# A seventh pair of up tiles through seven half products, with its weight sums kept in DRAM, and three moves in VectorE's order

## The chip, the cores and the metric

The kernel runs on one NeuronCore of a Trainium2 chip. TensorE (PE) multiplies into PSUM, VectorE (DVE) and ScalarE (ACT) work on PSUM and SBUF, GpSimd (POOL) scales the softmax, and SyncE (SP) issues nearly all DMAs. The metric is the device time of one execution in microseconds (us), the median of several runs.

## What is computed

One layer: forgetting attention on 512 tokens of width 1024 with 16 heads, a layer norm, a gated MLP of inner width 2816 with a causal convolution of three taps on its gate, a second layer norm, and a gated per-layer embedding. Everything is float32. The part that the change touches most is the MLP:

```python
def conv_ffn(x, w_up, conv_w, conv_b, w_down):
    u, g = jnp.split(x @ w_up, [FFN_DIM], axis=-1)
    g = causal_dwconv(g, conv_w, conv_b)
    return (jax.nn.gelu(g, approximate=False) * u) @ w_down
```

and, for the two smaller edits, the softmax of attention: `pr = softmax(q k^T * scale + c_q - c_k)` under a causal mask, then `pr @ v`.

## The kernel before

**Precision.** Each float32 operand is cut into a high and a low part (`whi`, `wlo` for weights; ACT makes the high part at line 123, DVE the low part at line 129), and each product is three matmuls (`three`, line 147). The class `Weights` (line 64) holds a list of units of up to 128x1024 weights in the order of use. A call `W.get(i, ahead)` cuts the units up to `i + ahead` and starts loads behind them; in the MLP `ahead` is 4, so DVE's work on a unit stands in its order four units ahead of the unit's matmuls. Raw weights rotate through four buffers, cut ones through five.

**The MLP.** The 22 tiles of inner width (`f`) come in 11 pairs (`j`). A plain pair makes, for each of its two tiles, the gate `g` and the up product `u` with 24 matmuls of 512 columns each (`up`, line 704); `conv` (line 714) follows on the gate, `product` (line 724) on both. A pair in `UP_PAIRS` is made by Winograd's form of Strassen's algorithm (`up_step`, line 751): seven products of halves instead of eight, for `g` (s = 0) and for `u` (s = 1), in four steps. Steps 0, 1 and 2 have 24 matmuls of 256 columns for each s, step 3 has 12. At step 0 ACT copies one product to a side buffer (`c1`) and zeroes its half bank, and DVE adds the two products (line 781); step 1 accumulates into that bank, so it waits for this add. `conv_product` (line 798) does both convolutions and both products after step 3.

The form needs sums and differences of blocks of the weights. For pairs not in `KEPT` they are made when the weights are cut: `t12` (two subtractions of 128x512, lines 207 and 208), `t3` and `t4` (one each, lines 215 and 222). For pairs in `KEPT` they are made during attention, written to DRAM and read back: `keep_load` (line 399) writes a finished set and loads the next raw blocks, `keep_sums` (line 413) makes four subtractions on DVE. There are two such rounds for a pair. They stand before the first head and behind `scores(h)` of even heads.

**Down products.** The down product goes by the same algorithm over groups of three pairs (`PAIRS`): part 0 is pairs 0 to 2, part 1 is 3 to 5, part 2 is 6 to 8; the rest is done plainly. While part p's up tiles are made, the down product of part p-1 runs in slices, called here d0 to d11 (`down`, line 825). Three slices make a phase: d0 to d2 use rows of the three pairs for the banks x and y, d3 to d5 and d6 to d8 use sums for z and x, d9 to d11 use one block for x. A slice has 12 matmuls of 512 columns (six in the last phase). At the end of a phase DVE adds the finished banks into `y` (`give`, line 849; two adds to a bank), and x is free for the next phase after that. `between` (line 875) takes the next slices: in parts 1 and 2 one at each of four places in a pair, in part 3 in turn two and one (`CHUNKS`, line 32). In a pair made of halves these places are behind step 0 of g, step 0 of u, step 1 and step 2.

The down product needs sums of a pair's products (`operand_sums`, four DVE additions, lines 814 to 817) and their high and low parts (`operand_parts`, three ACT copies and three DVE subtractions, lines 822 and 823: `a`, `b` and `s`). If the next pair is in `APART` (line 40), these are put into the next pair: the sums into step 0 of u ahead of its add, the parts behind it.

**Order.** From tile 2 on, DVE and ACT keep the order of the program text (`manual_schedule`, line 883). PE and SP are ordered by the compiler, which takes ready instructions out of the text's order. Ahead of that, in attention, DVE is ordered by the compiler as well, but `keep_sums` is tied behind the last mask instruction and the masks of odd heads behind the last sum (`issue_after`, lines 418 and 486).

**PSUM.** Six banks (`six`) serve the down product, two (`two`) the up tiles from tile 6 on. So a gate of tile f+1 waits until `conv(f)` has read the gate of tile f.

**Attention.** The loop at line 582 runs over h. Each turn has the scores of head h, a projection for a later head, the transposes P^T of head h-1 (`turn`, line 503; DVE writes the low part `PTl` at line 516) and the values of head h-2 (`values`). The layer's input `y` is loaded at h = 14, into the buffer that the last projection frees.

Of the kernel before, what the change touches and what calls it, by code (L numbers as in the profile page):

```python
# [19 lines left out]
H = 16  # L20
# [10 lines left out]

CHUNKS = (None, (1,) * 12, (1,) * 12, (2, 1) * 4)

UP_PAIRS = (2, 3, 4, 6, 7, 9)

KEPT = (3, 4, 6, 7)

DMA_PAIRS = (1, 2)

APART = (2, 3, 4, 7)  # L40
HALF = S // 2
ALPHA = 2.0 ** 0.25
EPS = 1e-5
# [99 lines left out]
def trunk_layer(ctx: ExitStack, tc: tile.TileContext, xT, x2d, pT, wqk, wv0, wv1, wv2, bf, wo, wup, cwb,  # L143
# [112 lines left out]
    for part in range(4):  # L256
# [3 lines left out]
        for i in range(2 * len(fs)):  # L260
            f, q = fs[i // 2], i % 2
            j, n = f // 2, i % 4
            if j in UP_PAIRS:
                stages = up_units(j)
# [4 lines left out]
            for _ in range(CHUNKS[part][i] if part else 0):  # L269
                if todo:  # L270
                    src, c, make = todo.pop(0)
                    u_dn[part - 1].append(W.add(src, n=c, inner=512, make=make))
            if j in UP_PAIRS and n == 3:
                for sq in range(2):
# [124 lines left out]
    def keep_load():  # L399

        if made:
            to, ab = made.pop()
            for n, t in enumerate(ab):
                nc.sync.dma_start(to[:, 2 * n:2 * n + 2, :], t.rearrange("p (a b) -> p a b", b=512))
        if to_keep:
            (j, q), to = to_keep.pop(0)
            ab = (ap.tile([P, UNIT], F32, name=f"ka{j}_{q}", tag="keep", bufs=1),
                  base.tile([P, UNIT], F32, name=f"kb{j}_{q}", tag="raw", bufs=RAW_BUFS))
            for n, t in enumerate(ab):
                nc.sync.dma_start(t.rearrange("p (a b) -> p a b", b=P), wup[2 * j + n, 1 - q])  # L410
            in_work.append((to, ab))

    def keep_sums():

        if in_work:
            behind = ExitStack()
            if last_mask:
                behind.enter_context(tc.issue_after(last_mask[0]))
            to, ab = in_work.pop()
            b11, b21, b12, b22 = [t[:, c:c + 512] for t in ab for c in (0, 512)]  # L420
            nc.vector.tensor_sub(b11, b12, b11)
            nc.vector.tensor_sub(b12, b22, b12)
            nc.vector.tensor_sub(b22, b22, b11)
            last_sum[:] = [nc.vector.tensor_sub(b21, b21, b22).ins]
            behind.close()
            made.append((to, ab))
# [91 lines left out]
    def values(h):  # L518
        m, j2 = divmod(h, 2)
        th, tl = PTh[h % 2], PTl[h % 2]  # L520
        ps = bank(f"o{h}")
        for j in range(NT):
            q0, o, w = PT[j]
            for n, p in enumerate((th, tl)):
                nc.tensor.matmul(ps[:, q0:], V[:, j, h], p[:, o:o + w], start=j == 0 and n == 0,  # L525
                                 stop=j == NT - 1 and n == 1)
        a = slice(j2 * 64, j2 * 64 + 64)
        if j2 == 0:
            outs[m] = ap.tile([P, S], F32, tag="o", name=f"o_{m}", bufs=1)
        o = outs[m]  # L530
        nc.scalar.activation(o[a], ps[64:], AF.Copy)
        nc.vector.tensor_add(o[a], ps[:64], o[a])
        if j2 == 1:
            nc.scalar.activation(oh[:, m, :], o, AF.Copy)
            nc.vector.tensor_sub(ol[:, m, :], o, oh[:, m, :].bitcast(F32))
# [46 lines left out]
    for h in range(H + 2):  # L582
        m, s = divmod(h, 2)
        if h == 2:
            project(2, 0)
        if h < H:
            scores(h)

            if s == 0:
                keep_sums()  # L590
                keep_load()
        if m + 1 < KD and h != 2:
            project(m + 1, s)
        for k in OUT_FIRST.get(h, ()):
            out_first(k)
        if s == 1 and h + 1 < H:
            stack(h + 1)
        if 1 <= h < H + 1:
            turn(h - 1)
        if h >= 2:  # L600
            values(h - 2)
        if s == 1 and h + 1 < H:
            stack(h + 2)
        if h == H - 2:
            y = base.tile([P, NT, D], F32, tag="xh", name="y")
            for t in range(NT):
                nc.sync.dma_start(y[:, t, :], x2d[t * P:(t + 1) * P, :])
# [96 lines left out]
    def up(f, s, c=slice(0, S), amid=None):  # L704
        if (f, s) not in ups:
            ups[f, s] = bank(f"{'gu'[s]}{f}", "two" if f >= 6 else None)
        hi, lo = W.get(u_up[f, s], 4 if f > 1 else 2)
        for k in range(KD):
            w = slice(k * P, (k + 1) * P)
            three(ups[f, s][:, c], hi[:, w], lo[:, w], x1h[:, k, c], x1l[:, k, c], k == 0, k == KD - 1)  # L710
            if amid is not None and k == 3:
                flip(*amid)

    def conv(f):

        pg = ups.pop((f, 0))
        a = gates[f] = hpool.tile([P, S], F32, tag="a", name=f"a{f}", bufs=2)
        nc.scalar.activation(a, pg, AF.Identity, bias=cw[:, f, 3:4], scale=cw[:, f, 2:3])
        nc.vector.scalar_tensor_tensor(a[:, 1:], pg[:, :S - 1], cw[:, f, 1:2], a[:, 1:],
                                       op0=ALU.mult, op1=ALU.add)  # L720
        nc.vector.scalar_tensor_tensor(a[:, 2:], pg[:, :S - 2], cw[:, f, 0:1], a[:, 2:],
                                       op0=ALU.mult, op1=ALU.add)
# [148 lines left out]
    for part in range(4):  # L871
        ops = []
        slots = iter(CHUNKS[part] or ())

        def between():
            for _ in range(next(slots, 0)):
                next(before)

        for f in range(6 * part, min(6 * part + 6, NF)):
            q, j = f % 2, f // 2  # L880
            if f == 2:

                ordered.enter_context(tc.manual_schedule(
                    engines={mybir.EngineType.DVE, mybir.EngineType.Activation}))
            if q == 0 and j not in APART:
                E = hpool.tile([P, 8 * HALF], F32, tag="E", name=f"E{j}")
            if f == 0:
                a, b = slice(0, HALF), slice(HALF, S)
                up(0, 0, a)
                up(0, 1, a)  # L890
                up(1, 0, a, (3, x1h, x1l, xt))
                up(0, 0, b)
                up(0, 1, b)
                up(1, 0, b)
                conv(0)
                product(0, E[:, :S])
                continue
            if j in UP_PAIRS:
                if q == 0:
                    up_step(j, 0, 0, E)  # L900
                    between()
                    up_step(j, 0, 1, E, (lambda: operand_sums(E)) if j in APART else None)
                    if j in APART:
                        operand_parts(pending.pop(), E)
                        E = hpool.tile([P, 8 * HALF], F32, tag="E", name=f"E{j}")
                    between()
                    continue
                for st in (1, 2):
                    up_step(j, st, 0, E)
                    up_step(j, st, 1, E)  # L910
                    if st == 1:
                        between()
                between()
                up_step(j, 3, 0, E)
                up_step(j, 3, 1, E)
                conv_product((f, f - 1), E)
            else:
                if f > 1:
                    up(f, 0)
                conv(f)  # L920
                between()
                up(f, 1)
                product(f, E[:, q * S:(q + 1) * S])
            if f == 1:
                x_sums()
            if q:
                if part < 3:
                    ops.append([cut_tiles("A", 2, 3, f"a{j}"), cut_tiles("B", 1, 5, f"b{j}", pool=hpool),
                                cut_tiles("S", 4, 4, f"s{j}")])
                    if j + 1 in APART:  # L930
                        pending.append(ops[-1])
                    else:
                        operand_sums(E)
                        operand_parts(ops[-1], E)
                else:
                    h, l = cut_tiles("S", 4, 4, f"s{j}")
                    e = E[:, :2 * S].rearrange("p (a b) -> p a b", b=HALF)
                    last_cut[:] = [nc.scalar.activation(h, e, AF.Copy).ins]
                    nc.vector.tensor_sub(l, e, h.bitcast(F32))
                    ops.append((h, l))  # L940
            if j not in UP_PAIRS:
                between()
        if part < 3:
            before = down(part, ops)
# [127 lines left out]
```

## Time and profile before

| | |
|---|---|
| Three runs | 653.12 to 653.72 us, median 653.72 |
| The profiled execution | 653.87 us; its span in the trace 652.1 us |
| PE, PE weight loads | 644.8 us busy (99%), 568.7 us (87%) |
| DVE, ACT, POOL | 521.2 us (80%), 367.3 us (56%), 93.0 us (14%) |
| DMA | 109.56 MB, mean 168 GB/s |
| Longest groups on DVE | low parts of weights, 90 of 128x1024, 109.7 us |

A timeline row has start, duration, engine, line, operation, tile out and in, and in brackets the idle time ahead of it and what ended it. Durations of rows that follow each other on one engine overlap a little, so start to start is the better measure of what an instruction costs its engine. The chain of waits is the work that ended last, followed back from the end; a row there has start, duration, engine, tile and line.

In this execution pair 7 ends on PE at 467.82, tiles 16 and 17 (pair 8, plain) run with d8 to d11 until 497.06, and pair 9 (halves, sums made on DVE) with d0 to d5 of the next part until 533.62.

### The profile page before, as it was taken

The numbers are of one execution on the slowest core, as the hardware profiler recorded it, in microseconds if no ns is written. First come the engines' busy times: TensorE is split into PE (matmuls) and PEld (weight loads), VectorE is DVE, ScalarE is ACT, GpSimd is POOL, SyncE is SP. The second block draws the span as 40 slices with busy tenths as digits, with TensorE's granted clock in tenths as the row PEclk, the third lists the DMA queues.
The fourth block names the chain that finished last, engine by engine and source line by source line (L and its number), as shares of the span: only waits on it lengthen the run. The fifth ranks groups of instructions, "written<-read, shape, count | busy, mean of one in ns | idle before, by whom it ended". The sixth has DMA issues, their size and how long they took to land.

```text
span 652.1 us, 10003 instructions
## 1 busy us (share of the span) xinstructions
PE 644.8 (99%) x3666; PEld 568.7 (87%) x3666; DVE 521.2 (80%) x854; ACT 367.3 (56%) x643; POOL 93.0 (14%) x85
## 2 busy tenths in 40 slices
PE   8999999999999999999999999999999999999997
PEld 8899888888888889889999988999978998888886
DVE  6764789988886599857899887799788998599464
ACT  6643777877785326946657564646545554425231
POOL 0000554454455021110000000000000000011000
PEclk9999999999999999999999999999999999999999
DMA  8763554555586215675655546564644473551321
GB/s 293 238 232 131 206 205 160 178 187 149 184 268 238 87 57 160 130 198 179 191 192 178 178 133 208 170 193 123 227 135 156 149 228 99 189 191 40 132 80 50
DMA packets 45858, 109.56 MB, mean 168 GB/s; under 512 B 4400, under 2 KB 8240, under 8 KB 45808
## 3 DMA queue, kind: packets, MB, share of 16 engines
q1 hardware_dynamic: 44944, 105.77, 49.6%
q0 software_dynamic: 864, 3.15, 2.6%
q8 instruction: 29, 0.48, 0.3%
q14 instruction: 21, 0.17, 0.1%
HBM read 96.19 MB, written 10.49 MB: 164 GB/s over the span
## 4 chain that ended last, share of the span: by engine, by line
PE 92%; DVE 4%; ACT 1%; issue 1%; DMA 1%; SPq 0%; DVEq 0%; ACTq 0%
PE u L152 16%; PE g L152 16%; PE pp L152 14%; PE x L152 7%; PE gt L152 7%; PE pv L152 7%; PE r L152 3%; PE z L152 3%; PE ap L152 3%; PE ao L152 3%; PE o L525 3%; PE t L512 2%; PE y L152 2%; PE s L475 2%; PE pl L152 2%; PE s L477 1%
## 5 line engine op out<-in xcount | busy, mean ns | idle before, releaser
L123 ACT ACTIVATE whi<-raw 128x1024 fp32r<-128x1024 f32 (+4 forms) x135 | 125.6, 938 | 92.5 <-PE pv L152 13.7
L129 DVE TENSOR_TENSOR wlo<-raw,whi 128x1024 fp32r<-128x1024 f32 (+4 forms) x130 | 138.3, 1073 | 33.8 <-ACT whi L123 32.8
L499 POOL TENSOR_SCALAR pr<-pr,rl 128x128 f32<-128x128 f32 (+1 forms) x64 | 74.9, 1186 | 132.8 <-DVE rl L495 132.8
L638 POOL TENSOR_TENSOR mv<-mv,neghalf 128x1 f32<-128x1 f32 x8 | 11.6, 1445 | 347.8 <-DVE mv L637 324.1
L152 PE MATMUL g<-x1h,whi 128*128 128x256 f32 (+1 forms) x168 | 54.5, 324 | 0.0
L152 PE MATMUL g<-x1l,whi 128*128 128x256 f32 (+1 forms) x168 | 54.4, 324 | 0.0
L152 PE MATMUL g<-x1h,wlo 128*128 128x256 f32 (+1 forms) x168 | 54.3, 323 | 0.0
L152 PE MATMUL u<-x1l,whi 128*128 128x256 f32 (+1 forms) x160 | 52.9, 331 | 0.0
L152 PE MATMUL u<-x1h,wlo 128*128 128x256 f32 (+1 forms) x160 | 52.9, 331 | 0.0
L152 PE MATMUL u<-x1h,whi 128*128 128x256 f32 (+1 forms) x160 | 52.9, 331 | 0.0
L152 PE MATMUL pp<-xh,wlo 128*128 128x512 f32 x128 | 50.6, 395 | 0.8 <-DVE PTl L516 0.8
L152 PE MATMUL pp<-xl,whi 128*128 128x512 f32 x128 | 50.0, 391 | 0.0
L152 PE MATMUL pp<-xh,whi 128*128 128x512 f32 x128 | 50.0, 391 | 0.0
L491 ACT ACTIVATE pr<-s,nm 128x128 f32<-128x128 f32 (+1 forms) x64 | 33.6, 528 | 10.4 <-DVE nm L487 10.3
L152 PEld LDWEIGHTS g<-x1l,whi 128*128 128x128 f32 x168 | 32.0, 190 | 2.7
L152 PEld LDWEIGHTS g<-x1h,whi 128*128 128x128 f32 x168 | 31.9, 190 | 2.7
L152 PEld LDWEIGHTS g<-x1h,wlo 128*128 128x128 f32 x168 | 31.9, 190 | 2.5
L152 PEld LDWEIGHTS u<-x1h,whi 128*128 128x128 f32 x160 | 30.4, 190 | 3.0
L152 PEld LDWEIGHTS u<-x1l,whi 128*128 128x128 f32 x160 | 30.4, 190 | 3.0
L152 PEld LDWEIGHTS u<-x1h,wlo 128*128 128x128 f32 x160 | 30.4, 190 | 2.8
L487 DVE CUSTOM_DVE_ANT_0 s<-s,mask 128x128 f32<-128x128 f32 (+1 forms) x64 | 30.0, 512 | 1.7 <-PE s L477 1.5
L123 ACT ACTIVATE whi<-side 128x512 fp32r<-128x512 f32 (+1 forms) x33 | 25.5, 782 | 9.7 <-PE u L152 3.6
(550 smaller groups left out, 1820.2 us busy)
## 6 DMA issues: line engine op xcount, KB each, us to landing
raw<-wup SPq DMA_DIRECT2D x34, 512.0 KB, 3.5
raw<-wdn SPq DMA_DIRECT2D x23, 512.0 KB, 3.9
raw<-wqk SPq DMA_DIRECT2D x16, 512.0 KB, 3.4
ka<-wup SPq DMA_DIRECT2D x8, 512.0 KB, 3.9
kb<-wup SPq DMA_DIRECT2D x8, 512.0 KB, 3.4
kept<-kb SPq DMA_DIRECT2D x8, 512.0 KB, 3.5
kept<-ka SPq DMA_DIRECT2D x8, 512.0 KB, 3.1
raw<-wo SPq DMA_DIRECT2D x8, 512.0 KB, 4.1
```

The source lines that it names most:

```text
L123: self.nc.scalar.activation(hi[:, c:e], piece, AF.Copy)
L129: self.nc.vector.tensor_sub(lo[:, c:e], piece, hi[:, c:e].bitcast(F32))
L152: nc.tensor.matmul(ps, lhsT, rhs, start=start and n == 0, stop=stop and n == 2, skip_group_check=on)
L475: nc.tensor.matmul(ps[:, :n], QA[:, q], KA[:, :n], start=True, stop=False)
L477: nc.tensor.matmul(ps[:, :n], qb[0:68, q], kb[0:68, :n], start=False, stop=True)
L487: last_mask[:] = [nc.vector.tensor_tensor_reduce(ps[:, :w], ps[:, :w], mask[:, S - w:], -1.0, BIG, op0=ALU.add, op1=ALU.min, accum_out=nm[ ...
L491: nc.scalar.activation(pr[:, off:off + w], ps[:, :w], AF.Exp, bias=nm[:, i:i + 1], scale=-1.0, accum_out=ls[:, i:i + 1])
L499: nc.gpsimd.tensor_scalar_mul(pr[:, off:off + w], pr[:, off:off + w], rl[:, i:i + 1])
L512: nc.tensor.transpose(ps[:, w:w + P], pr[:, o:o + P], ident)
L525: nc.tensor.matmul(ps[:, q0:], V[:, j, h], p[:, o:o + w], start=j == 0 and n == 0, stop=j == NT - 1 and n == 1)
L638: nc.gpsimd.tensor_tensor(mv[:, 3:4], mv[:, 2:3], neghalf, op=ALU.pow)
```

## The change

Pair 8 (tiles 16 and 17, the last pair of part 2) joins `UP_PAIRS` and `KEPT`. Pairs 8 and 9 join `APART`, so the sums and parts of pair 7 stand in pair 8 and those of pair 8 in pair 9. Two more rounds of sums are kept: the sums of the first new one stand at h = 14, and `keep_sums` and `keep_load` are called once more at h = 16, where the load of `y` now stands too. For h = 2 the round moves from behind the scores to behind `turn` and `values`. And in a plain tile whose slice ends a phase, `conv` stands behind that slice and its adds into `y`. With pair 8 gone from the plain ones, this holds for tile 10 alone (slice d8 of part 1); tile 11 has d10, and tiles 20 and 21 of part 3 have d6, d7 and d9, d10 there.

```diff
-UP_PAIRS = (2, 3, 4, 6, 7, 9)
+UP_PAIRS = (2, 3, 4, 6, 7, 8, 9)
-KEPT = (3, 4, 6, 7)
+KEPT = (3, 4, 6, 7, 8)
-APART = (2, 3, 4, 7)
+APART = (2, 3, 4, 7, 8, 9)
...
-            if s == 0:
+            if s == 0 and h != 2:
                 keep_sums()
                 keep_load()
...
         if h >= 2:
             values(h - 2)
+        if h in (2, H):
+            keep_sums()
+            keep_load()
         if s == 1 and h + 1 < H:
             stack(h + 2)
-        if h == H - 2:
+        if h == H:
             y = base.tile([P, NT, D], F32, tag="xh", name="y")
...
-                conv(f)
+
+                n = 4 * (j - 3 * part) + 2 * q
+                late = part and any(sum(CHUNKS[part][:n], i) % 3 == 2 for i in range(CHUNKS[part][n]))
+                if not late:
+                    conv(f)
                 between()
+                if late:
+                    conv(f)
                 up(f, 1)
```

## The prediction

> **What bounds the kernel now.** I read the page's busy shares first, then the stretches of the MLP around pair 8, then the chain of waits, then DVE's timeline.
>
> ```profile
> PE 644.8 (99%) x3666; PEld 568.7 (87%) x3666; DVE 521.2 (80%) x854; ACT 367.3 (56%) x643; POOL 93.0 (14%) x85
> 467.84:475.80 7.96, 7.96 (x36) 6.57 (x35) 6.45 (x13) 4.49 (x8) 0.00 (x0) 1.00 0.32 105
> 475.80:497.06 21.26, 20.86 (x93) 16.97 (x92) 16.79 (x24) 9.70 (x13) 0.00 (x0) 1.00 0.62 194
> 497.06:505.40 8.34, 8.34 (x51) 7.38 (x50) 8.12 (x13) 5.29 (x9) 0.00 (x0) 1.00 0.25 72
> 505.40:513.90 8.50, 8.50 (x63) 8.01 (x62) 8.39 (x15) 4.46 (x8) 0.00 (x0) 1.00 0.65 191
> 513.90:533.62 19.72, 19.72 (x133) 18.27 (x133) 19.45 (x29) 10.23 (x15) 0.00 (x0) 1.00 0.60 198
> ```
>
> A stretch has its length, then busy us of PE, weight loads, DVE, ACT and POOL, then granted clock, DMA share and GB/s. The kernel is bound by PE, and PE's clock is full (1.00). But the last three rows, pair 9, show a second limit: there DVE is busy for 35.96 of 36.56 us. Fewer matmuls help only where DVE still serves PE in time. In pair 8 (the two rows before) DVE has 29.22 - 23.24 = 6.0 us to spare.
>
> **Matmuls of pair 8.**
>
> ```profile
> 466.36 1.46 PE u L152 x12
> 490.26 5.44 PE u L152 x24
> 497.06 2.87 PE g L152 x24
> 532.18 1.44 PE u L152 x12
> 508.28 1.39 PE x L152 x6
> 509.66 1.36 PE y L152 x6
> 481.40 0.61 DVE y L627
> 482.05 1.64 PE x L152 x6
> 483.69 5.21 PE g L152 x23
> ```
>
> These are rows of the chain. Plain, the pair is 4 x 5.44 = 21.76 us. As halves it is 6 x 2.87 + 2 x 1.44 = 20.10 us: **-1.66**. The slices d8 to d11 are five runs of six (1.36 each, 6.8 us) either way. So 21.76 + 6.8 = 28.56 us of matmuls took 497.06 - 467.82 = 29.24 us: 0.68 us is lost where x of d9 waits for the add into `y` of d8 (481.40, then 482.05).
>
> The Trainium skill, "TensorE: Matmul & The Clock Gate", section "Back-to-back issue gap", gives an isolated gap of N/2.4 + 2.5 ns; by it the 168 half matmuls against 96 whole ones would save an estimated 2.4 us. The rows (0.120 and 0.227 us a matmul) decide for the smaller saving.
>
> **DVE behind pair 7, in pair 8.** DVE keeps the text's order, so its queue can be written out.
>
> ```profile
> 468.96 0.75 DVE L719 SCALAR_TENSOR_TENSOR a<-E,cw,a 128x511 f32<-128x511 f32 x1 [0.93 <-ACT a L718]
> 473.71 0.42 DVE L814 TENSOR_TENSOR E<-E 128x256 f32<-128x256 f32 x1
> 475.19 0.69 DVE L823 TENSOR_TENSOR a7l<-E,a7h 128x512 fp32r<-128x512 f32 x1
> 477.54 0.68 DVE L222 TENSOR_TENSOR raw<-raw,side 128x512 f32<-128x512 f32 x1
> 478.14 1.22 DVE L129 TENSOR_TENSOR wlo<-side,whi 128x1024 fp32r<-128x1024 f32 x1
> 479.28 0.74 DVE L719 SCALAR_TENSOR_TENSOR a<-g,cw,a 128x511 f32<-128x511 f32 x1
> 480.72 0.68 DVE L129 TENSOR_TENSOR wlo<-raw,whi 128x512 fp32r<-128x512 f32 x1
> 481.32 1.28 DVE L627 TENSOR_TENSOR y<-y,x 128x512 f32<-128x512 f32 x2
> 482.51 1.28 DVE L627 TENSOR_TENSOR y<-y,z 128x512 f32<-128x512 f32 x2
> ```
>
> Start to start: `conv_product` runs to 473.7, 5.85 us behind PE's end of the pair (467.82); sums 1.45, parts 2.35 (475.19 to 477.54); a weight's low part 1.14, of half size 0.60 (480.72 to 481.32); a `t4` 0.60; two adds into `y` 1.2; a `conv` 1.44 (479.28 to 480.72); the add at line 781 0.34 (below). From PE's end T of pair 7 the new order is: conv_product to T+5.85, a low part 7.0, add for g 7.3, t4 and low part 9.05, four adds of d8 11.45, a half low part 12.05, sums 13.5, add for u **T+13.85**. Step 1 of u waits for the last. Until then PE has step 0 of g and u, d8, d9 and step 1 of g: 3 x 2.87 + 2.72 + 1.36 = 12.7 us. d10 can't fill, its operand is among the deferred parts. So PE idles **+1.15**, where it now loses 0.68. Bounds: 0 (adds and cuts land earlier), 2.4 (the four adds in full). The three extra units to cut (3.4 us) fit into DVE's 6.0 us: my order reaches the last cut at PE's end plus 1.1, just when `conv_product` can start. They cost nothing while it does; if it doesn't, what exceeds comes on top in pair 9.
>
> **DVE behind pair 8, in pair 9.**
>
> ```profile
> 500.36 1.22 DVE L129 TENSOR_TENSOR wlo<-raw,whi 128x1024 fp32r<-128x1024 f32 x1
> 502.69 0.69 DVE L207 TENSOR_TENSOR raw<-raw,side 128x512 f32<-128x512 f32 x1
> 505.15 0.42 DVE L781 TENSOR_TENSOR E<-g,side 128x256 f32<-128x256 f32 x1
> 505.49 0.68 DVE L207 TENSOR_TENSOR side<-side 128x512 f32<-128x512 f32 x1
> 513.08 0.42 DVE L781 TENSOR_TENSOR E<-u,side 128x256 f32<-128x256 f32 x1
> 525.75 0.68 DVE L792 TENSOR_TENSOR E<-g,E 128x512 f32<-128x512 f32 x1
> ```
>
> Today step 1 of u starts at 513.90 (the stretch's border) and its add begins at 513.08: 0.4 us of slack. Between the two adds stand three units with `t12`, 2.53 us each (505.49 to 513.08). New, from PE's end T' of pair 8: conv_product to 5.85, `t12` and a low part 2.46 (502.69 to 505.15), add for g 8.65, three units 16.2, sums 17.7, add for u **T'+18.05**, then the part `a` of pair 8 at 18.65, which d2 needs. Until 18.05 PE has step 0 of g and u and step 1 of g (8.6), d0 and d1 (5.44) and z of d3 (1.36): 15.4 us. So PE idles **+2.6** at least, if the compiler pulls step 1 of g and z of d3 ahead of d2. It does such things: the run of g at 483.69 has 23 matmuls, since the first of the 24 was set ahead of x at 482.05, where the text has x first. Behind it all adds and cuts come in time by the same count (the add for g of 525.75, now due at T'+33, against its need at 36). In text order d2 would be met at T'+11.2 and wait for 18.65: 7.4. Bounds 0 and 7.4; I take 2.6, and +0.4 for an order that was made by a model of DVE.
>
> The Trainium skill, "TensorE: Matmul & The Clock Gate", in the table at its head (row "Engine queue depth"), says that DVE and ACT are strict FIFO and that PE pulls only weight loads ahead. DVE's rows above, all in the text's order, agree. By it the chip mends nothing that the compiled order has wrong.
>
> **Tile 10.**
>
> ```profile
> 389.80 1.28 DVE L627 TENSOR_TENSOR y<-y,x 128x512 f32<-128x512 f32 x2
> 390.53 1.66 PE x L152 x6
> ```
>
> x of d9 takes 1.66 instead of 1.36 and starts some 0.1 us late, behind the add of 389.80. With `conv` (1.44) behind the adds, they start at 388.36: **-0.4**. Queued behind these four adds (2.4), `conv` ends at 392.2; the gate of tile 11 needs the bank that it reads and could run from about 391.4 (x from 390.1, for 1.36). d10 (1.36 us, operands ready) can fill that; if not, +0.8 and a net +0.4.
>
> **Third head.**
>
> ```profile
> 85.87 0.69 DVE L421 TENSOR_TENSOR ka<-kb,ka 128x512 f32<-128x512 f32 x1
> 87.69 0.66 DVE L422 TENSOR_TENSOR kb<-kb 128x512 f32<-128x512 f32 x1
> 89.01 0.50 PE L152 MATMUL pp<-xh,wlo 128*128 128x512 f32 x1 [0.84 <-DVE PTl L516]
> ```
>
> Two sums (0.7 each) run in the 2.4 us ahead of `PTl`, for which PE idles 0.84. Moved behind: **-0.8**. The masks of head 3 then queue behind all four sums, about 1 us later, and the round's stores and loads on SP move back as well, with two heads' time until the next round wants them. Bounds -0.9 and +0.3.
>
> **Two more rounds.**
>
> ```profile
> 195.50 1.23 DVE L129 TENSOR_TENSOR wlo<-raw,whi 128x1024 fp32r<-128x1024 f32 x1
> 198.44 1.61 DVE L129 TENSOR_TENSOR wlo<-raw,whi 128x1024 fp32r<-128x1024 f32 x1 [1.62 <-ACT whi L123]
> 199.97 1.61 DVE L516 TENSOR_TENSOR PTl<-t,PTh 128x512 fp32r<-128x512 f32 x3
> 218.44 1.23 DVE L129 TENSOR_TENSOR wlo<-raw,whi 128x1024 fp32r<-128x1024 f32 x1 [2.28 <-ACT whi L123]
> 225.10 1.28 DVE L625 SCALAR_TENSOR_TENSOR y<-y,ao 128x512 f32<-128x512 f32 x2 [0.82 <-PE ao L152]
> ```
>
> Each is four subtractions (2.6 us) on DVE. At h = 14 a gap of 1.62 covers part, so `PTl` of 199.97 comes about 1 us late; PE has output-projection matmuls to put there. At h = 16 there are gaps like the 2.28 ahead of 218.44. SP gets four loads and four stores of 512 KB, and the four loads of `y` may now stand behind a store that waits for the sums; `y` is first wanted at 225.10, some 8 us after those. Taken **+0.2**, bounds 0 and 2.6. In the MLP the pair reads 3.5 MB instead of 2 MB (3.5 units of 512 KB for each of g and u, not two), at a DMA share of 0.25 to 0.65 in the stretches above: nothing.
>
> **Sum.** -1.66 - 0.68 + 1.15 + 2.6 + 0.4 - 0.4 - 0.8 + 0.2 = +0.8. The profiled execution took 653.87 (span 652.1), 0.15 above the median of the runs; to the median this is **654.5**.
>
> **Rivals.**
> - *DVE's delay stays hidden.* The idle 1.15 + 2.6 + 0.4 goes to zero: 650.4. For it: PE has lost only 0.4 us to DVE in the whole MLP (the stretch 475.80:497.06, 20.86 of 21.26, and nothing in pair 9). Against: at 513.08 the slack is only 0.4; behind the pair's start that add now comes 1.7 us later, and d2 (2.72) can't run ahead of it any more, only z of d3 (1.36) in its place.
> - *Slower: d2 keeps its place.* If the compiled order leaves d2 ahead of step 1 of g, PE waits 7.4 instead of 3.0: 658.9. It decides where the model has part `a` of pair 8 ready more than some 3 us too early. Against: the gate matmul at 482.05 puts that model within about half a us.
> - *The end of attention.* The rounds at h = 14 and 16 cost their 2.6 us in full: 656.9.
> - *Only the matmuls and the third head count*, tile 10 gives back 0.5 and pair 8 idles 2.4: 656.6, taken with the rival before.
>
> **How the numbers follow.** Forecast 0.42 (652.5 to 656.5), hidden delay 0.28, d2 in place 0.17, the last two 0.13. A difference under 0.2% (1.3 us) can't be told from no change here. Faster takes all of the hidden delay and a little of the forecast: 0.30. The forecast's middle is same: 0.33. Its upper part and the other two are slower: 0.37. The range goes from the hidden delay to d2 in place, 650.2 to 658.9.
>
> **What would show it.** The pair's rows: 24 matmuls in 2.87, not 5.44. In pair 8, PE idle for about 1 us ahead of step 1 of u, released by DVE at line 781 for u; in pair 9 about 3 us, by the same line or by `a8l`, with DVE without a gap from `conv_product` to that add. Step 1 of g ahead of d2 tells the forecast from text order. The 0.84 at `pp` and the restart at tile 10 should be gone. I'd be wrong if DVE stood well ahead at PE's end of pair 8, or if the sums of pair 8 ran before the three units with `t12`.

## Result, and the profile after

The changed kernel takes a median of 655.75 us (nine runs, 654.92 to 656.3) against 653.72 (nine runs, 653.12 to 654.17) of the kernel before: a ratio of 1.003, 95% interval 1.0019 to 1.004. It is slower by 2.0 us. The profiled execution took 655.2 us with a span of 653.5, so the two traces differ by 1.4; the other 0.6 is only in the medians, and no single trace shows it.

The page's first part, after (engine, busy us, share, instructions):

```profile
PE 643.6 (98%) x3738; PEld 570.3 (87%) x3738; DVE 530.3 (81%) x870; ACT 373.5 (57%) x661; POOL 94.2 (14%) x85
```

TensorE is busy for 1.2 us less than before, as fewer products should give, and the kernel is longer. So the loss is idle time of PE. The stretches of pairs 8, 9 and 10, after (start and end, length, then busy us of PE, weight loads, DVE, ACT and POOL, granted clock, DMA share, GB/s):

```profile
467.36:495.07 27.71, 27.45 (x200) 25.86 (x200) 23.62 (x36) 17.95 (x31) 0.00 (x0) 1.00 0.59 192
495.07:534.91 39.84, 37.46 (x242) 33.49 (x241) 39.17 (x60) 22.99 (x39) 0.00 (x0) 1.00 0.55 179
534.91:572.00 37.09, 37.06 (x163) 30.37 (x163) 28.75 (x37) 17.79 (x23) 0.00 (x0) 1.00 0.47 150
```

Pair 8 took 29.24 us and now takes 27.71. Pair 9, whose 242 matmuls are the same, took 36.56 and takes 39.84. DVE is busy for 39.17 of those 39.84 us: it got 3.2 us more work than before (35.96), and the pair became 3.3 us longer. In pair 10 DVE is busy for 28.75 of 37.09. The waits of PE, after (who waits for what, us in total, times, longest):

```profile
PE u L152 <- DVE side L784: 1.4, 1, 1.4
...
PE s L475 <- DVE KA L462: 0.8, 1, 0.8
PE x L152 <- ACT a8h L825: 0.5, 1, 0.5
PE g L152 <- DVE wlo L129: 0.5, 1, 0.5
PE x L152 <- DVE y L630: 0.3, 1, 0.3
PE pp L152 <- DVE PTl L516: 0.2, 1, 0.2
```

Three of them lie in pair 9: the add for u (line 784, 781 before), part `a` of pair 8 (`a8h`) and a weight's low part. They are 2.4 of its 3.3 us. From start to start of the matmuls another 0.5 goes at these three places, and 0.4 is spread over the pair. `KA` is new, in head 3. The 0.84 at `pp` is down to 0.2.

Where the 1.4 us between the traces comes from, by the same places in PE's order in both:

| part | predicted | in the traces |
|---|---|---|
| third head (PE's run of `pp` at 108.30 before, 108.42 after) | -0.8 | +0.1 |
| the rest of attention, with two more rounds (to 248.81 and 248.55) | +0.2 | -0.4 |
| tile 10 (its pair, 5, with d8 to d11: 28.99 and 28.80) | -0.4 | -0.2 |
| pair 8 (29.24 and 27.71) | -1.2 | -1.5 |
| pair 9 (36.56 and 39.84) | +3.0 | +3.3 |
| behind | 0 | +0.1 |
| sum | +0.8 | +1.4 |

The first row counts from the start of the trace. PE is 0.1 us ahead already at the scores of head 2 (83.54, before 83.64), so from there the third head reads +0.2.

The start of pair 9 on DVE, after, in its timeline (start, duration, engine, line, operation, tiles, idle ahead):

```profile
493.18 1.23 DVE L129 TENSOR_TENSOR wlo<-raw,whi 128x1024 fp32r<-128x1024 f32 x1 [1.62 <-ACT whi L123]
...
497.79 0.74 DVE L722 SCALAR_TENSOR_TENSOR a<-E,cw,a 128x511 f32<-128x511 f32 x1
...
504.60 0.42 DVE L784 TENSOR_TENSOR side<-g,side 128x256 f32<-128x256 f32 x1
...
513.99 0.41 DVE L784 TENSOR_TENSOR side<-u,side 128x256 f32<-128x256 f32 x1
```

PE ends pair 8 at 495.07. `conv_product` starts on DVE 2.72 us later, the add for g at 504.60, the add for u at 513.99, and from the start of `conv_product` to that add DVE has one gap, of 0.16. The chain of waits of the same stretch, after (start, us, engine, tile, line), shows how one full queue reaches PE:

```profile
502.06 1.38 PE y L152 x6
...
503.46 1.22 DVE wlo L129
504.68 0.34 DVE side L784
...
513.65 0.42 DVE E L820
514.07 0.34 DVE side L784
...
514.46 0.86 PE u L152 x5
```

From 503.46 to 514.46 it is DVE alone, instruction behind instruction. The chain calls some pieces of it "issue" (two of 0.57 are the longest), time in which the profile shows no wait; DVE's timeline has no gap there. What starts at 514.46 is step 1 of u.

### The profile page after: what moved, and what is told of

Same layout as the page of the kernel before. It is cut to its first block, busy times and chain, and to the rows that moved or that the text cites. A ratio compares the mean times of both kernels' runs of the same rounds, so it can differ in the third digit from the quotient of the medians.

```text
span 653.5 us, 10213 instructions
## 1 busy us (share of the span) xinstructions
PE 643.6 (98%) x3738; PEld 570.3 (87%) x3738; DVE 530.3 (81%) x870; ACT 373.5 (57%) x661; POOL 94.2 (14%) x85
## 4 chain that ended last, share of the span: by engine, by line
PE 91%; DVE 5%; ACT 1%; issue 1%; DMA 1%; SPq 0%; DVEq 0%; ACTq 0%
PE u L152 17%; PE g L152 17%; PE pp L152 13%; PE x L152 7%; PE gt L152 7%; PE pv L152 7%; PE r L152 3%; PE z L152 3%; PE ap L152 3%; PE o L525 2%; PE ao L152 2%; PE t L512 2%; PE y L152 2%; PE pl L152 2%; PE s L475 2%; PE s L477 1%
## 5 line engine op out<-in xcount | busy, mean ns | idle before, releaser
L123 ACT ACTIVATE whi<-raw 128x1024 fp32r<-128x1024 f32 (+4 forms) x138 | 127.8, 934 | 89.5 <-issue 14.0
L152 PE MATMUL g<-x1h,whi 128*128 128x256 f32 (+1 forms) x164 | 51.8, 316 | 0.0
L152 PE MATMUL g<-x1l,whi 128*128 128x256 f32 (+1 forms) x164 | 51.6, 314 | 0.0
L152 PE MATMUL g<-x1h,wlo 128*128 128x256 f32 (+1 forms) x164 | 51.6, 314 | 0.0
L152 PE MATMUL u<-x1l,whi 128*128 128x256 f32 (+1 forms) x156 | 50.1, 321 | 0.0
L152 PE MATMUL u<-x1h,wlo 128*128 128x256 f32 (+1 forms) x156 | 50.1, 321 | 0.0
L152 PE MATMUL u<-x1h,whi 128*128 128x256 f32 (+1 forms) x156 | 50.1, 321 | 0.0
L152 PE MATMUL u<-xsh,whi 128*128 128x256 f32 x112 | 31.8, 284 | 1.4 <-DVE side L784 1.4
L152 PE MATMUL g<-xsh,wlo 128*128 128x256 f32 x112 | 31.8, 284 | 0.5 <-DVE wlo L129 0.5
L152 PE MATMUL g<-xsh,whi 128*128 128x256 f32 x112 | 31.8, 284 | 0.0
```

What stands on the lines that cost most here:

```text
L123: self.nc.scalar.activation(hi[:, c:e], piece, AF.Copy)
L152: nc.tensor.matmul(ps, lhsT, rhs, start=start and n == 0, stop=stop and n == 2, skip_group_check=on)
```

## Experiments

The theory after the profile: pair 9 pays, since DVE is late there, and the third head gave nothing. Open were three things: whether pair 9 is all of it; whether the fault there is the **order** of DVE's instructions (an early one stands behind others that could wait) or their **amount**; and why the third head gave nothing. Ratios are to the kernel before, run beside each; its median there was 653.72 beside the changed kernel, 654.06 beside `pair8_plain`, `rounds_alone`, `head3_back` and `no_apart9`, 653.87 beside `part_a_early`, `add_first`, `both_early` and `head3_untied`, 653.91 beside `pool_t12` and `plain_untied`, and 653.48 beside the last two.

| run | median us | ratio, 95% interval |
|---|---|---|
| changed kernel | 655.75 | 1.003 (1.0019 to 1.004) |
| `pair8_plain` | 653.69 | 0.9993 (0.9985 to 1.0002) |
| `rounds_alone` | 653.8 | 0.9995 (0.9986 to 1.0003) |
| `head3_back` | 655.41 | 1.002 (1.0011 to 1.0028) |
| `no_apart9` | 655.31 | 1.0024 (1.0012 to 1.0035) |
| `part_a_early` | 657.12 | 1.0045 (1.0032 to 1.0057) |
| `add_first` | 655.97 | 1.0029 (1.0017 to 1.004) |
| `both_early` | 657.12 | 1.0048 (1.0035 to 1.006) |
| `head3_untied` | 654.66 | 1.0011 (1.0002 to 1.002) |
| `pool_t12` | 661.06 | 1.0111 (1.0096 to 1.0127) |
| `plain_untied` | 652.82 | 0.9984 (0.9975 to 0.9992) |
| `leave_t12` | 653.91 | 1.0004 (0.9995 to 1.0013) |
| `chunks_untied` | 654.81 | 1.002 (1.0011 to 1.0029) |

**Parts of the change.** The diffs are against the changed kernel.

`pair8_plain`: pair 8 plain again, the other moves stay.

```diff
-UP_PAIRS = (2, 3, 4, 6, 7, 8, 9)
+UP_PAIRS = (2, 3, 4, 6, 7, 9)
-KEPT = (3, 4, 6, 7, 8)
+KEPT = (3, 4, 6, 7)
-APART = (2, 3, 4, 7, 8, 9)
+APART = (2, 3, 4, 7)
```

> Pair 8 plain as before, with its two rounds gone, the old APART; the other edits stay (third head's round behind the values, the load of y at h = 16, conv behind the phase's adds, now for tiles 10 and 16). If the halves of pair 8 and what hangs on them are the whole loss (queue on DVE in pair 9), this is at or a little below before: third head 0 (the trace of after shows its gain spent again by 108.4), tile 10 -0.2, tile 16 up to -0.6, so 652.9 to 653.5. If the small edits themselves cost, it stays at 655 to 656.

653.69 is 0.2 us above the range expected. Its median lies below the changed kernel's by 2.1 us, its ratio by 0.37% (2.4 us): pair 8 as halves, with what it moves into pair 9, is the loss, and the other edits by themselves can't be told from no change.

`rounds_alone`: of the change only the two more rounds.

```diff
-UP_PAIRS = (2, 3, 4, 6, 7, 8, 9)
+UP_PAIRS = (2, 3, 4, 6, 7, 9)
-APART = (2, 3, 4, 7, 8, 9)
+APART = (2, 3, 4, 7)
...
-            if s == 0 and h != 2:
+            if s == 0:
...
-        if h in (2, H):
+        if h == H:
...
-                late = part and any(sum(CHUNKS[part][:n], i) % 3 == 2 for i in range(CHUNKS[part][n]))
+                late = False and any(sum(CHUNKS[part][:n], i) % 3 == 2 for i in range(CHUNKS[part][n]))
```

> Only the two more rounds of sums (h = 14 and 16, with their loads, stores and the later load of y) are added to the kernel before; their sums are written and not read, pair 8 is plain. If the rounds are hidden, as the trace of after has it (PE leaves attention 0.3 us earlier than before), 653.4 to 654.0. If the rounds in attention are the cost, 655 to 656.

The rounds are hidden: 0.9995, with an interval that ends at 1.0003. The rival that priced them at 2.6 us in full is out.

`head3_back`: the round of h = 2 behind the scores again.

```diff
-            if s == 0 and h != 2:
+            if s == 0:
...
-        if h in (2, H):
+        if h == H:
```

> The changed kernel with the third head's round back behind the scores. By the trace of after the gain of 0.7 at the first projection behind it is lost again where the scores of a later head wait for KA: then this is within 0.3 of the changed kernel, 655.4 to 656.0. If the move is worth the 0.8 of the prediction, 656.5.

655.41 beside 655.75, with intervals that overlap: no gain of the move can be seen. The trace tells why. The first fence is DVE's timeline of before, the second of after.

```profile
89.94 0.69 DVE L424 TENSOR_TENSOR ka<-ka,kb 128x512 f32<-128x512 f32 x1
...
91.60 0.28 DVE L487 CUSTOM_DVE_ANT_0 s<-s,mask 128x128 f32<-128x128 f32 x1
```

```profile
92.42 0.69 DVE L424 TENSOR_TENSOR ka<-ka,kb 128x512 f32<-128x512 f32 x1
93.14 0.30 DVE L487 CUSTOM_DVE_ANT_0 s<-s,mask 128x128 f32<-128x128 f32 x1
```

The last sum comes at 92.42, not 89.94, and the masks of head 3 are tied behind it (line 486), so they start 1.5 us later. Their exponentials and the `KB` copy follow on ACT, then `KA` on DVE. The chain of after:

```profile
88.31 0.96 PE pp L152 x3
...
96.42 0.49 ACT KB L459
...
96.94 0.69 DVE KA L462
...
97.67 0.50 PE s L475 x2
```

PE resumes at 88.31, not at 89.01 (0.1 us of this it had already ahead of head 2), and then waits 0.8 us for `KA`.

`head3_untied`: the masks of head 3 may run ahead of the last sum.

```diff
-            if h % 2 and last_sum:
+            if h % 2 and last_sum and h != 3:
```

> The changed kernel with the masks of head 3 no longer tied behind the last sum of the third head's round. If the tie is what loses the 0.7 again (masks, then ACT's exponentials and copies, then KA), 654.9 to 655.3. If the loss comes from ACT's order or the round's DMAs, no change: 655.5 to 656.0.

1.0011 against 1.003, and 1.1 us between the medians. In its trace the sums stand between the masks, no wait for `KA` is left, and PE reaches the run of `pp` that stood at 108.42 here:

```profile
107.64 2.52 PE pp L152 x11
```

That is 0.7 us ahead of the kernel before (108.30), near the 0.8 that the move was priced at: it gains once the tie does not take it back. The tie loosened with the round at its old place was not run; in the trace of before it holds nothing up, since two other instructions of DVE stand between the last sum (89.94) and the first mask (91.60).

`plain_untied` is `pair8_plain` with this edit.

> Pair 8 plain and its rounds gone, as in the run of that kind before, and the masks of head 3 not tied behind the sums. What the loosened tie gained on the changed kernel (1.1 in the median, 0.8 in the trace) it gains here too: 652.6 to 653.1, faster than before. If that gain was drift between chips, 653.5 to 653.9.

652.82, ratio 0.9984 (0.9975 to 0.9992): the only variant whose interval lies below the kernel before. The gain is small, 0.16%.

**Order of DVE in pair 9.** `no_apart9`: the sums and parts of pair 8 stand behind `conv_product` again, not inside pair 9.

```diff
-APART = (2, 3, 4, 7, 8, 9)
+APART = (2, 3, 4, 7, 8)
```

> The changed kernel with pair 9 taken out of APART: the sums and all parts of pair 8 stand right behind its products, ahead of the three units with t12. If the add for u is what PE waits for, it comes later by the parts that now stand ahead of it (2.2), but d2 (2.7) can run before it: pair 9 idles 2.8 to 4.0 instead of 3.3, total 655.2 to 656.4. If putting pair 9 in APART is the fault by itself, the 3.3 of pair 9 go and it is 652.5.

655.31, not to be told from the changed kernel. The wait for the add of u is gone, and two others stand in its place. Waits of PE in `no_apart9`:

```profile
PE x L152 <- DVE wlo L129: 1.5, 1, 1.5
PE z L152 <- DVE wlo L129: 1.2, 1, 1.2
```

`part_a_early`: part `a` of pair 8, for which d2 waits, ahead of step 0 of pair 9.

```diff
+                    if j == 9:
+                        operand_parts(pending[-1], E, slice(0, 1))
...
-                        operand_parts(pending.pop(), E)
+                        operand_parts(pending.pop(), E, slice(j == 9, 3))
```

> The changed kernel with part a of pair 8 (one ACT copy, one DVE subtraction; it needs no sums) ahead of step 0 of pair 9. Queue theory: d2 can run before the add for u, which comes 0.6 later, so PE has 18.1 us of work until the add at 19.9 behind pair 8's end: idle 3.3 becomes 1.2 to 2.0, total 653.7 to 654.6. If DVE's amount of work in pair 9 sets the time and not its order, no change: 655.4 to 656.1.

657.12, slower. DVE itself now stands still for 0.70 us at this place, as its timeline in `part_a_early` shows, and the waits of PE there follow:

```profile
502.83 0.69 DVE L826 TENSOR_TENSOR a8l<-E,a8h 128x512 fp32r<-128x512 f32 x1 [0.70 <-ACT a8h L825]
```

```profile
PE u L152 <- DVE side L784: 1.2, 1, 1.2
...
PE z L152 <- DVE wlo L129: 0.7, 1, 0.7
```

These waits are shorter together than those of the changed kernel in pair 9 (1.9 and 2.4 us). What turns it into a loss is the clock: behind the wait for the add, the 24 matmuls of step 1 of u take 4.62 us instead of 2.87, at a granted clock of 0.63 (chain and stretch in `part_a_early`; in the changed kernel the clock is 1.00 there). These 1.7 us are more than the 1.4 between the medians.

```profile
515.77 4.62 PE u L152 x24
515.77:520.38 4.61, 4.61 (x25) 4.61 (x26) 4.15 (x7) 3.65 (x7) 0.00 (x0) 0.63 0.07 18
```

All five runs of `part_a_early` list a mean clock of 0.996 or 0.997, the nine of the changed kernel 0.999 or 1.000. Why it fell here, behind a wait of 1.2 us, and not behind the 1.4 us of the changed kernel, no run shows.

`add_first`: the add for u ahead of the four sums, in all pairs of `APART`. `both_early`: this and the edit before.

```diff
+            nc.vector.tensor_add(c1 if j in APART else e[:, :HALF], x, c1)
             if amid is not None:
                 amid()
-            nc.vector.tensor_add(c1 if j in APART else e[:, :HALF], x, c1)
```

> The changed kernel with the add of step 0 for u ahead of the four sums, in all pairs of APART. Queue theory: the add for u comes 1.45 earlier, in pair 9 idle 3.3 becomes 1.9 to 2.5, in pair 8 0.8 becomes 0 to 0.5, total 654.0 to 654.9. If DVE's amount of work sets the time, no change: 655.4 to 656.1.

> Both moves together. Queue theory: the add for u at about 18.5 behind pair 8's end, 18.1 us of work on PE before it: pair 9 idles 0.3 to 1.0, total 652.2 to 653.2, below before. If the amount of DVE's work sets the time, 655.4 to 656.1.

655.97 and 657.12: misses, both. The wait for the add of u is gone in both, and PE waits elsewhere. Waits of PE in `both_early`:

```profile
PE z L152 <- DVE wlo L129: 1.8, 2, 1.0
...
PE g L152 <- ACT E L789: 0.8, 3, 0.3
```

From pair 9's first matmul to pair 10's, PE takes 36.55 us in the trace of before and 39.83 in that of after. The four orders have:

| run | pair 9, us | beside it |
|---|---|---|
| `no_apart9` | 40.05 | |
| `part_a_early` | 40.68 | some 1.7 us of it by the lower clock (4.62 - 2.87) |
| `add_first` | 39.11 | pair 8 takes 28.08, not 27.73: its step 2 waits for ACT's copies |
| `both_early` | 40.63 | pair 8 takes 28.07; the clock is 1.00 |

The best saves 0.7 us there, and `part_a_early` would have saved an estimated 0.9 at full clock (40.68 - 1.74, against 39.83). So the order counts for a part, but none of the four comes near the 3.3 us: what is put first is served, and other waits come up. That fits a full queue better than one badly placed instruction. How much the amount of work does, they don't measure.

**Amount of DVE's work in pair 9.** `pool_t12`: the ten `t12` subtractions for the two units of pair 9 and for d3 to d5 on POOL, which is idle there.

```diff
-    def t12(b11, i):
+    def t12(b11, i, eng=nc.vector):
...
-            nc.vector.tensor_sub(t1, t1, t2)
-            nc.vector.tensor_sub(t2, t[:, 512:], t1)
+            eng.tensor_sub(t1, t1, t2)
+            eng.tensor_sub(t2, t[:, 512:], t1)
```

> The changed kernel with the ten subtractions of t12 for pair 9's units and for d3 to d5 beside them on POOL instead of DVE; the order of DVE stays. If the amount of DVE's work in pair 9 sets the time (the three reorderings moved PE's waits from one unit to the next and gained nothing), DVE has 4 x 1.33 = 5.3 us less ahead of the add for u and 6.7 less in the pair: PE's 3.3 us of idle time in pair 9 go, total 652.2 to 653.0. If POOL is too late with them (two of up to 2 us each for a unit) or holds DVE up, 655 to 658.

661.06, by far the slowest. POOL's timeline and DVE's in `pool_t12`:

```profile
497.86 1.29 POOL L207 TENSOR_TENSOR raw<-raw,side 128x512 f32<-128x512 f32 x1 [216.22 <-DMA raw<-wup]
499.23 1.61 POOL L208 TENSOR_TENSOR side<-raw 128x512 f32<-128x512 f32 x1
500.80 1.74 POOL L207 TENSOR_TENSOR raw<-raw,side 128x512 f32<-128x512 f32 x1
...
509.37 2.14 POOL L208 TENSOR_TENSOR side<-raw 128x512 f32<-128x512 f32 x1
...
521.97 1.30 POOL L208 TENSOR_TENSOR side<-raw 128x512 f32<-128x512 f32 x1
```

```profile
497.84 1.86 DVE L724 SCALAR_TENSOR_TENSOR a<-E,cw,a 128x511 f32<-128x511 f32 x1
499.73 1.66 DVE L726 SCALAR_TENSOR_TENSOR a<-E,cw,a 128x510 f32<-128x510 f32 x1
...
508.08 2.29 DVE L129 TENSOR_TENSOR wlo<-raw,whi 128x1024 fp32r<-128x1024 f32 x1
510.29 0.41 DVE L786 TENSOR_TENSOR side<-g,side 128x256 f32<-128x256 f32 x1
```

While POOL works, DVE's instructions with two operands in SBUF take about twice as long, and the add for g ends 5.7 us later than in the changed kernel; PE waits 4.4 us for it. Behind that wait the granted clock is 0.50 from 510 to 515 and 0.85 from 515 to 520, so a part of the 5.3 us between the medians is the clock. This run took no time off DVE ahead of the two adds, so it says nothing on the amount.

`leave_t12` asks the same question without POOL.

```diff
-    def t12(b11, i):
+    def t12(b11, i, summed=True):
...
-            nc.vector.tensor_sub(t1, t1, t2)
-            nc.vector.tensor_sub(t2, t[:, 512:], t1)
+            if summed:
+                nc.vector.tensor_sub(t1, t1, t2)
+                nc.vector.tensor_sub(t2, t[:, 512:], t1)
...
-            [(b_rows(j, 0, 2, 1), UNIT, t12(wdn[2 * j * P:(2 * j + 1) * P, 0:512], i))
+            [(b_rows(j, 0, 2, 1), UNIT, t12(wdn[2 * j * P:(2 * j + 1) * P, 0:512], i, part != 2))
...
-        return (lambda q: unit(f0, q), lambda q: unit(f1, q, t12(wup[f0, 1 - q][:, :4], 3 + q)),
+        return (lambda q: unit(f0, q), lambda q: unit(f1, q, t12(wup[f0, 1 - q][:, :4], 3 + q, j != 9)),
```

> Left out: the ten subtractions t12 (0.6 us each start to start, some 6 us of DVE) of the two units of pair 9 and of the slices d3 to d5 of part 2, whose blocks go unsummed into the matmuls; DVE's order, PE's matmuls and the loads are those of the changed kernel. Theory (DVE's amount of work in pair 9, 39.17 of 39.84 us, sets its length): the 3.3 us that pair 9 lost come back, 652.0 to 653.3, and PE's waits for wlo and for the add of u go below 1 us together. Rival (something else sets it: raw weights that land late, a buffer, the compiled order): 654.8 to 656.

653.91, ratio 1.0004: between the two ranges expected. 1.8 us come back in the medians (1.7 by the ratios), a little over half of what pair 9 lost. The stretch of pair 9 and the only wait of PE in it, in `leave_t12`:

```profile
495.50:533.37 37.87, 37.11 (x242) 33.78 (x241) 34.61 (x52) 22.59 (x39) 0.00 (x0) 1.00 0.60 196
```

```profile
PE x L152 <- DVE a8l L827: 0.8, 1, 0.8
```

Pair 9 takes 37.87 us, between 36.56 and 39.84. DVE has 3.3 us to spare, and the waits for the add of u and for weights are gone. So the work taken out accounts for 2.0 of the 3.3 us. Eight of the ten subtractions stood ahead of the add for u, which now ends at 509.70, 14.2 us behind the end of pair 8 instead of 19.3: the run takes work out of the pair and shortens the queue to that add at once, and does not part the two. Of the 1.3 that stay, most is d2's wait for part `a` with its restart (1.0 from start to start); that part still stands behind `conv_product`, the cuts and the sums, so here the place in the queue does count. Whether moving it forward pays once DVE has room was not tried, and stays open.

`chunks_untied`: the changed kernel with head 3 untied, and two slices moved from pair 9 into pair 10.

```diff
-CHUNKS = (None, (1,) * 12, (1,) * 12, (2, 1) * 4)
+CHUNKS = (None, (1,) * 12, (1,) * 12, (1,) * 4 + (2,) * 4)
```

> The changed kernel with the masks of head 3 untied (654.66 by itself) and part 3's slices shared out as 1,1,1,1 in pair 9 and 2,2,2,2 in pair 10, not 2,1 four times: the two slices d4 and d5, their four t12 subtractions, two low parts and the adds behind d5 leave pair 9, where DVE is full, for pair 10, where DVE is busy for 28.75 of 37.09 us. Theory (amount of work on DVE in pair 9): most of pair 9's 3.3 us comes back, 651.3 to 652.5. Rival (the order at the pair's start, conv_product and the add for u, sets it): no gain over 654.7, or a loss, as PE has fewer slices to fill with, up to 657.

654.81, no gain over `head3_untied`. Waits of PE in `chunks_untied`:

```profile
PE g L152 <- ACT E L799: 1.1, 1, 1.1
PE x L152 <- DVE y L630: 1.1, 2, 0.8
...
PE u L152 <- DVE side L784: 0.7, 1, 0.7
```

The wait for u halves, from 1.4 to 0.7, as less DVE work stands ahead of it. But a wait for an ACT copy of pair 8's last product is new, ahead of pair 9's first gate matmul at 495.24, and another in pair 10, where x waits at 545.32 for adds into `y`. The edit moved more than the amount, so its time, which is that of the rival, decides nothing; only the halved wait speaks for the theory.

## Why the prediction came out as it did

The likeliest case was the right one: 655.75 lies in the upper part of its 652.5 to 656.5, and neither the hidden delay (650.4) nor d2 in text order (658.9) happened. Its middle was +0.8; the traces have +1.4 and the medians +2.0. The largest miss is one term, and two of the terms that came out well did so partly by luck.

- **Pair 9, +3.0: right, +3.3.** The prediction counted DVE's queue from the end of pair 8, T', to the add for u at T'+18.05, against 15.4 us of matmuls. The add ended at 514.40, T'+19.3, and PE had 16.5 (19.4 to the start at 514.46, less 2.9 of idle from start to start). Place and releaser were as forecast; that the size came out so well is luck, since two errors cancel. `conv_product` began at T'+2.72, not T'+1.1. DVE had stood idle for 1.62 at 493.18, since ACT's cut of that unit waited for PE (ACT's timeline and PE's, after):

```profile
492.09 1.06 ACT L123 ACTIVATE whi<-raw 128x1024 fp32r<-128x1024 f32 x1 [2.38 <-PE x L152]
```

```profile
510.83 0.74 PE L152 MATMUL x<-whi,a8h 128*128 128x512 f32 x2 [0.48 <-ACT a8h L825]
511.41 0.63 PE L152 MATMUL y<-whi,a8h 128*128 128x512 f32 x2
```

- And PE took these four matmuls of d2 ahead of step 1 of u, while the low part of `a` was still to come; the count had left them out. Step 1 of g and z of d3 did run ahead of the rest of d2, as forecast.
- **What it named and did not use**: it called the row "35.96 of 36.56" a second limit, but then priced the idle as the lateness of one add, where 3.2 us of new work for DVE came into a pair with 0.6 us to spare. Four other orders of the queue didn't save it; less work on DVE took back 2.0 of the 3.3.
- **Pair 8, -1.2: -1.5.** The matmuls went as priced. "d10 can't fill, its operand is among the deferred parts" was wrong. The deferred parts are those of pair 7 (`a7`), while d10 uses `b4`. PE's timeline, after:

```profile
480.46 0.40 PE L152 MATMUL x<-whi,b4h 128*128 128x512 f32 x1
```

- d10 ran there, and the add for u, at T+14.1 (forecast T+13.85), made nobody wait. The stall at x of d9, priced as gone, stayed. So the idle time forecast ahead of step 1 of u stood at another place and was smaller, and the near agreement is luck. The chain, after:

```profile
476.76 0.61 DVE y L630
...
477.41 1.66 PE x L152 x6
```

- **Third head, -0.8: +0.1 in the trace, no gain in `head3_back`.** This is the term that failed. The prediction said that the masks would be "about 1 us later" and gave +0.3 as the far bound, yet summed the gain in full. The masks came 1.5 us later, and PE waited 0.8 us for `KA` behind them; with the masks untied the gain was there.
- **Tile 10, -0.4: -0.2.** d10 filled the gap as said. The chain, after:

```profile
389.94 2.27 PE x L152 x10
392.20 5.65 PE g L152 x24
```

- x waits for nothing and runs ten matmuls, six of d9 and four of d10; the gate behind it takes 5.65, not the 5.44 of a full run.
- **Two rounds, +0.2: hidden**, by `rounds_alone`. The -0.4 of the table is no gain that can be put down to them: for the same part of attention the traces with the rounds have 140.05 to 140.15 us, those without (before, `pair8_plain`, `plain_untied`) 139.96 to 140.51.

## What to carry to other kernels

Where a second engine is busy for 98% of a stretch, work moved into that stretch can cost the first engine as much time (3.2 us moved in, 3.3 lost here), and other orders of the queue need not give it back (the best of four gave 0.7 in its pair, and nothing in the total); look for work to take out, and first ask what a deferred step will find in the stretch that receives it. Read the granted clock before comparing waits: in `part_a_early` the waits fell and the time rose. When an instruction is moved later, follow whatever is tied behind it up to the next thing that PE needs: the gain at the old place is only the first half of the sum.

## What the runs showed of the hardware

POOL and DVE slow each other down in fp32 work from SBUF to SBUF. Beside POOL's subtractions of 128x512, DVE's operations of 128x511 and 128x510 took 1.66 to 1.86 us instead of 0.75, a low part of 128x1024 2.29 instead of 1.23; POOL's subtractions took 1.3 to 3.0. From 499 to 506 both engines start an instruction every 1.6 to 1.8 us, in step. An add with one operand in PSUM took 0.41 at 510.29, beside POOL's of 509.37, as always. The Trainium skill, "SBUF — State Buffer", section "SBUF: two separate sides", says that DVE and GpSimd share a port pair, that a DVE operation with two SBUF inputs takes it against a GpSimd operation that reads SBUF, and that the one that starts first gets it for its whole instruction while the other blocks. The rows agree that the two engines take turns: from 499 to 506 each start on one falls between two on the other. They don't settle the length of a turn: the POOL subtraction at 521.97, beside DVE adds with an operand in PSUM, took 1.30, and 1.30 + 0.75 is more than the 1.6 to 1.8 between starts. Idle time on POOL was no room for DVE's work here.
